# The attention branch's projection from fp16 parts, and another order of the steps ahead of it

## The chip, the cores and the metric

The kernel runs on one core of a Trainium2 chip. A core has a matrix engine (TensorE, "PE" in the profile), a vector engine (VectorE, "DVE"), a scalar engine (ScalarE, "ACT"), a general engine (GpSimd, "POOL") and a sync engine (SyncE, "SP") that here only issues transfers. Each works through its own queue of instructions in order, and semaphores tie the queues together. Operands lie in an on-chip memory of 128 partitions (SBUF); TensorE writes its sums to a second one (PSUM), from which DVE or ACT fetch them. The metric is the device time of one execution in microseconds; lower is better.

## The reference

One layer of an encoder on 1024 tokens of width 1024, all in float32. Cut to what matters:

```python
h = rmsnorm(x, norm_gain)
q, k, v, gate_a, u_in, v_in, gate_b, g_merge = split(h @ w_in)
attn = block_attention(rope(rmsnorm(q)), rope(rmsnorm(k)), v) * silu(gate_a)
y_a = attn @ w_proj_attn                                   # 512 -> 1024
vv = layernorm(gelu(v_in), ln_v_gain, ln_v_bias)
gm = gelu(u_in) * (w_spatial . vv + b_spatial) * silu(gate_b)
y_b = gm @ w_proj_gmlp                                     # 512 -> 1024
g = sigmoid(g_merge + b_merge)                             # two gates of 1024
y = g[0] * y_a + g[1] * y_b
out = rmsnorm(x + y @ w_out, final_gain)
```

There are 8 query heads and 2 key/value heads of width 64, and the attention looks at all 1024 tokens. The change concerns `y_a = attn @ w_proj_attn`, and the order of everything up to there.

## The kernel before

**Parts.** Every product is made from two parts of each operand: a hi part, the value rounded to a narrower type, and a lo part, the rest. `mm3` (lines 183 to 186) issues three matmuls for each pair: hi by hi, hi by lo, lo by hi. In most of the kernel the parts are fp16. As fp16 has a small range, an operand is scaled first: its squares are summed on ACT (`activation(..., Square, accum_out=...)`), a small matmul sums them over the partitions, and POOL takes them to the power of -1/2 (`unit_scale`, line 276; `scales`, line 325). `split16` (line 288) then makes hi on ACT with that scale and lo on DVE with one instruction. The factor is taken out again where the product is used. In two places, the projections of the branches, the parts are fp32r, four bytes wide, and need no scale: `split` (line 127) rounds on ACT and subtracts on DVE.

**Stages.** (1) x is loaded and split, k and v are projected, then the input of the spatial mixer (`v_group`). (2) The weights of q are scaled and split (`prep_q`), x is normalised (`norm_part`) and split again (`norm_split`), q is projected (`q_group`), normalised and turned (`q_norm`), and transposed (`q_split`). (3) 64 steps of attention: `scores` makes the softmax of 128 queries of one head and sends its parts through a transposing DMA, `mix2` multiplies them with v. Between them stand 24 `run_fill`, the products for the gated paths u, a and b, each from weights that `prep_next` has loaded and split. Path a ends in `gat`, the gated attention, four tiles of two halves. (4) `proj_b`, 8 times: the other branch's projection, from a stream of weights, with its loads in the tiles `wraw`. (5) Eight gates (`gate`, line 984), and among them four times `proj_a` (line 988), the attention branch's projection, two blocks of 128 output rows at a time. (6) The output product with the residual and the last norm.

**The projection.** `proj_a` calls `proj_pair`, and that calls `seven`: a product of 2 by 2 blocks in seven products instead of eight, from sums and differences of the blocks. `make_forms` makes the seven forms of `gat`; `sums` those of the weights; the function `weights` inside `proj_pair` splits each form of 256 columns just before its product. Each product has two parts of the inner dimension, and so six matmuls of 128x512. When a projection and a gate for the same rows are there, `merge` (line 888) joins them with the branch b in `ys`. The squares of the result (line 997) go into the scale of the output product.

**Order.** The order of the calls from line 1001 on is written out by hand. The framework's planner takes it as a priority and puts each engine's instructions in order by its own estimate of when operands are ready; a tile with several buffers waits until one is free. The loads are issued on SP's queue in that order, those of the early scales on ACT's. The tiles `X`, `T16`, `rB` and `vS` hold the forms of `gat`; `wraw` has four buffers, which the loads of `scales`, `proj_b`, `proj_pair` and `square_out` share.

Of the kernel before, what the change touches and what calls it, by code (L numbers as in the profile page):

```python
# [30 lines left out]
def hybrid_block_kernel(  # L31
# [681 lines left out]

    def make_forms(q, n, alloc, B, e_sub, e_hi, e_lo):
# [59 lines left out]
    GAT = ("X", "X", "T16 T16", "T16 T16", "X", "X", "rB vS")  # L774
# [14 lines left out]

    def g_tile(key, i):  # L790
        if GAT[i] == "X":
            t = tX(f"gf{key}").rearrange("p k (j t) -> p k j t", j=2)
            return t[:, 0], t[:, 1]
        return [t4(GAT[i].split()[p], f"gf{key}{p}", F32R).rearrange("p (j t) -> p j t", j=2) for p in range(2)]

# [51 lines left out]
    def proj_pair(i, b, G, dst):  # L847
# [5 lines left out]
        def weights(key, raw):  # L853
            t = sb.tile([P, 2, 256], F32R, tag="wh", bufs=WHB, name=f"wp{b}{i}{key}")
            split(t[:, 0], t[:, 1], raw, act, WPL[count[0] % len(WPL)])
            count[0] += 1
            return t[:, 0], t[:, 1]
# [131 lines left out]
    def proj_a(i):  # L989
# [12 lines left out]
    qT = [qT2[j // 2][:, j % 2] for j in range(4)]  # L1002
    load_pair(1)
# [31 lines left out]
    early = scales(["q"] + order[:4], ["xa"] * 8)  # L1035
# [5 lines left out]
    for h in range(2):  # L1041
        dve.tensor_copy(rB[:, H(h)], rp[h])
    with tc.high_priority():
# [4 lines left out]
    load_wsp(0)  # L1048
    v_group(0)
    v_group(1)  # L1050
    load_pair(0)
    load_pair(3)
    prep_q(0)
    vss = const([P, 4], "vss")
    for h in range(2):
        act.activation(t2(f"vsq{h}"), vn[:, H(h)], AF.Square, accum_out=vss[:, h:h + 1])
    load_wsp(1)
    load_pair(2)
    scale_wsp()
    norm_part(5)  # L1060
    v_post(0)
    v_post(1)
    prep_q(1)
    ktmp = t4("vS", "ktmp")
    head_norm(kn, ktmp, 0, 8, "kf")
    norm_part(0)
    bias_term(0)
    v_group(2)
    prep_q(2)
    prep_q(3)  # L1070
    prep_q(4)
    norm_part(3)
    norm_part(2)
    v_group(3)
    rope(kn, ktmp, Ak, Bk, 8, 2)
# [9 lines left out]
    prep_q(5)  # L1085
# [4 lines left out]
    split(khl[0], khl[1], kn, act)  # L1090
    prep_q(6)
    v4 = vn.rearrange("p (t h d) -> p t h d", h=2, d=64)
    v_post(2)
    v_post(7)
    norm_part(7)
    norm_split(5)
    vS = sb.tile([P, 8, 2, 128], F16, tag="vS", bufs=1, name="vS")
    act.activation(vS[:, :, :, 0:64], v4, AF.Copy, scale=vss[:, 3:4])
    dve.scalar_tensor_tensor(out=vS[:, :, :, 64:128], in0=v4, scalar=vss[:, 3:4], in1=vS[:, :, :, 0:64],
                             op0=ALU.mult, op1=ALU.subtract)  # L1100
    v_post(3)
    norm_part(6)
    norm_split(2)
    k_transposes(1)
    norm_part(4)
    norm_split(6)
    v_post(4)
    norm_split(4)
    norm_part(1)
    spatial(0)  # L1110
    norm_split(7)
    k_transposes(2)
    norm_split(1)
    bias_term(1)
    prep_q(7)
    k_transposes(3)
    norm_split(0)
    norm_split(3)
    scales(order[4:6])
    q_group(0)  # L1120
    k_transposes(0)
    v_post(6)
    q_norm(0)
    v_post(5)
    spatial(1)
    q_split(1)
    q_split(0)
    q_group(3)
    spatial(3)
    q_group(1)  # L1130
    prep_next()
    spatial(2)
    prep_next()
    q_group(2)
    q_norm(1)
    scales(order[6:8])
    q_split(2)
    q_norm(2)
# [5 lines left out]
    q_split(3)  # L1144
    scores(*hs[3])
    prep_next()
    v_affine(1)
    q_norm(3)
    scores(*hs[4])
    v_affine(2)  # L1150
    run_fill(*halves[0])
    scores(*hs[5])
    scores(*hs[6])
    scores(*hs[7])
    q_split(4)
    q_split(5)
    prep_next()
    scores(*hs[8])
    scores(*hs[9])
    scales(order[8:10])  # L1160
    scores(*hs[10])
    scales(order[10:12])
    scores(*hs[11])
    q_split(7)
    q_split(6)
    mix2(*hs[0][:2])
    scores(*hs[12])
    mix2(*hs[4][:2])
    scores(*hs[13])
    prep_next()  # L1170
    run_fill(*halves[1])
    scores(*hs[14])
    scores(*hs[15])
    scores(*hs[16])
    run_fill(*halves[2])
    mix2(*hs[8][:2])
    scores(*hs[17])
    scores(*hs[18])
    mix2(*hs[12][:2])
    scores(*hs[19])  # L1180
    scores(*hs[20])
    scores(*hs[21])
    run_fill(*halves[3])
    scores(*hs[22])
    v_affine(0)
    scores(*hs[23])
    scores(*hs[24])
    scores(*hs[25])
    run_fill(*halves[4])
    run_fill(*halves[5])  # L1190
    prep_next()
# [3 lines left out]
    scores(*hs[26])  # L1195
    mix2(*hs[16][:2])
    mix2(*hs[20][:2])
    scores(*hs[27])
    run_fill(*halves[8])
    scores(*hs[28])  # L1200
    run_fill(*halves[9])
    v_affine(3)
    scores(*hs[29])
    scores(*hs[30])
    run_fill(*halves[10])
    scores(*hs[31])
    run_fill(*halves[11])
    prep_next()
    mix2(*hs[24][:2])
    run_fill(*halves[12])  # L1210
    mix2(*hs[28][:2])
    scores(*hs[32])
# [3 lines left out]
    scores(*hs[36])  # L1216
    scores(*hs[37])
    run_fill(*halves[13])
    run_fill(*halves[14])
    scores(*hs[38])  # L1220
    mix2(*hs[32][:2])
    scores(*hs[39])
    scores(*hs[40])
    prep_next()
    scores(*hs[41])
    prep_next()
    scores(*hs[42])
    scores(*hs[43])
    scores(*hs[44])
    scores(*hs[45])  # L1230
    scores(*hs[46])
    run_fill(*halves[15])
    scores(*hs[47])
    scores(*hs[48])
    mix2(*hs[36][:2])
    mix2(*hs[40][:2])
# [199 lines left out]
```

## Time and profile before

| | |
|---|---|
| runs | 709.68, 710.73, 712.04 us; median 710.73 |
| the profiled execution's own time | 715.41 us |
| its span, first to last instruction | 713.6 us |
| mean granted clock of TensorE | 0.986 |
| busy: PE, DVE, ACT, POOL | 686.7, 569.5, 480.1, 98.3 us |

The profile is of one execution. A line of it names engine, source line and operation, then the tiles that are written and read. A number pair behind a bar is the busy time of the group in us and the mean of one instruction in ns. "[2.59 <-DMA wraw]" is idle time of the engine before an instruction, with what ended it. Matmuls overlap, so a single one's duration is longer than the time from one to the next. In windows the granted clock is a share of full speed.

### The profile page before, as it was taken

What the parts mean: (1) busy time and instruction counts of PE and PEld (TensorE: products, weight loads), DVE (VectorE), ACT (ScalarE), POOL (GpSimd) and SP (SyncE); (2) the same over time, 40 slices, a digit from 0 to 9 for tenths busy, and PEclk for the clock granted to TensorE, in tenths of its full rate; (3) what the DMA queues carried; (4) which work ended last, traced back from release to release, by engine and by line L of the source; (5) the groups of instructions that cost most, each with busy time, mean ns of one, the idle gap of its engine ahead of it and who ended that gap; (6) DMA issues with size and microseconds to landing.
All of it is one profiled execution on the core that took longest, in us unless ns stands there. A gap on an engine that the chain in (4) does not pass through costs nothing.

```text
span 713.6 us, 12246 instructions
## 1 busy us (share of the span) xinstructions
PE 686.7 (96%) x4752; PEld 403.0 (56%) x4752; DVE 569.5 (80%) x820; ACT 480.1 (67%) x896; POOL 98.3 (14%) x118
## 2 busy tenths in 40 slices
PE   9899999989998999989999999999899999999996
PEld 8788745434555545545556885644545564444443
DVE  6469997799898997899788999888688897972233
ACT  6696788667897987788678597694674648831011
POOL 0014241353011111001101001011011102000000
PEclk9999999989999999999999999999999999999999
DMA  8993255334889998899997630520520043511202
GB/s 301 407 406 122 86 188 169 117 59 90 134 187 168 199 172 143 158 221 177 167 186 166 218 104 1 176 90 30 184 75 37 1 158 124 190 42 48 118 31 88
DMA packets 159818, 102.40 MB, mean 143 GB/s; under 512 B 136208, under 2 KB 136848, under 8 KB 159760
## 3 DMA queue, kind: packets, MB, share of 16 engines
q1 hardware_dynamic: 158320, 97.14, 53.0%
q10 hardware_dynamic: 1440, 4.47, 1.6%
q8 instruction: 37, 0.61, 0.4%
q14 instruction: 21, 0.17, 0.1%
HBM read 63.85 MB, written 4.19 MB: 95 GB/s over the span
## 4 chain that ended last, share of the span: by engine, by line
PE 55%; DVE 16%; DMA 12%; ACT 9%; issue 5%; SPq 1%; POOL 1%; POOLq 0%; ACTq 0%; DVEq 0%
DMA T<-p 6%; PE out L186 4%; PE out L185 4%; PE out L184 4%; DMA wraw<-in_wall_dram 3%; DVE p L651 3%; ACT p L650 3%; DVE nm L640 3%; PE g L184 3%; PE g L186 3%; PE g L185 3%; ACT P L644 3%; PE o L665 2%; PE yb L184 2%; PE yb L186 2%
## 5 line engine op out<-in xcount | busy, mean ns | idle before, releaser
L651 DVE SCALAR_TENSOR_TENSOR p<-P,ri,p 128x1024 f16<-128x1024 f32 x64 | 83.2, 1303 | 14.4 <-ACT p L650 13.8
L644 ACT ACTIVATE P<-s,nm 128x1024 f32<-128x1024 f32 x64 | 71.1, 1111 | 24.3 <-DVE nm L640 17.4
L640 DVE TENSOR_REDUCE nm<-s 128x1 f32<-128x1024 f32 x64 | 77.5, 1214 | 1.4 <-PE s L638 1.4
L650 ACT ACTIVATE p<-P,ri 128x1024 f16<-128x1024 f32 x64 | 72.9, 1142 | 7.8 <-DMA T<-p 5.0
L665 PEld LDWEIGHTS <-vS 128*64 128x64 f16 x1536 | 46.9, 113 | 20.3 <-issue 16.4
L665 PE MATMUL o<-T,vS 128*64 128x128 f16 x1536 | 52.5, 224 | 5.7 <-DMA T<-p 5.6
L637 PE MATMUL s<-kT,qT 128*128 128x512 f16 x128 | 49.6, 388 | 4.3 <-ACT qT L450 2.0
L638 PE MATMUL s<-kT,qT 128*128 128x512 f16 x128 | 49.5, 387 | 0.0
L185 PE MATMUL out<-wo,yhl 128*128 128x512 f16 (+2 forms) x136 | 49.5, 366 | 0.0
L186 PE MATMUL out<-wo,yhl 128*128 128x512 f16 (+2 forms) x136 | 49.3, 366 | 0.0
L184 PE MATMUL out<-wo,yhl 128*128 128x512 f16 (+2 forms) x136 | 48.8, 366 | 0.0
L956 ACT ACTIVATE sq<-xr 128x1024 f32<-128x1024 f32 x7 | 7.4, 1057 | 58.9 <-DVE xr L1365 58.5
L1365 DVE SCALAR_TENSOR_TENSOR xr<-out,osc,xr 128x1024 f32<-128x1024 f32 x7 | 9.0, 1284 | 40.8 <-PE out L186 40.8
L184 PE MATMUL g<-x,wg 128*128 128x512 f16 x96 | 36.4, 380 | 0.0
L185 PE MATMUL g<-x,wg 128*128 128x512 f16 x96 | 36.4, 379 | 0.0
L186 PE MATMUL g<-x,wg 128*128 128x512 f16 x96 | 36.3, 379 | 0.0
L282 POOL TENSOR_SCALAR scg<-scg 128x1 f32<-128x1 f32 x8 | 4.1, 513 | 194.3 <-ACT usg L281 194.3
L184 PE MATMUL yb<-gm,wh 128*128 128x512 f32 x64 | 25.4, 397 | 0.0
L184 PE MATMUL v<-nh,xhl 128*128 128x512 f32 x64 | 25.3, 395 | 0.0
L185 PE MATMUL v<-nl,xhl 128*128 128x512 f32 x64 | 25.2, 393 | 0.0
L596 POOL TENSOR_TENSOR vm<-vm,ut 128x512 f32<-128x512 f32 x8 | 14.4, 1804 | 77.3 <-DVE ut L369 42.7
L185 PE MATMUL yb<-gm,wh 128*128 128x512 f32 x64 | 24.9, 390 | 0.0
(566 smaller groups left out, 1933.5 us busy)
## 6 DMA issues: line engine op xcount, KB each, us to landing
wraw<-in_wall_dram SPq DMA_DIRECT2D x91, 256.0 KB, 3.3
graw<-in_wall_dram SPq DMA_DIRECT2D x16, 512.0 KB, 5.7
xraw<-in_xT_dram SPq DMA_DIRECT2D x13, 512.0 KB, 4.9
xn<-in_x_dram SPq DMA_DIRECT2D x8, 512.0 KB, 8.0
xp<-in_xT_dram SPq DMA_DIRECT2D x8, 512.0 KB, 7.9
wor<-in_wall_dram SPq DMA_DIRECT2D x8, 512.0 KB, 5.5
xr<-in_x_dram SPq DMA_DIRECT2D x8, 512.0 KB, 4.0
out_dram<-xr SPq DMA_DIRECT2D x7, 512.0 KB, 2.6
```

The lines of the kernel that those rows point to most:

```text
L184: pe.matmul(o, ah, bh, start=start, stop=False)
L185: pe.matmul(o, ah, bl, start=False, stop=False)
L186: pe.matmul(o, al, bh, start=False, stop=stop)
L596: pool.tensor_tensor(out=vm[:, et, H(h)], in0=vm[:, et, H(h)], in1=t, op=ALU.mult)
L637: pe.matmul(sp[:, H(hf)], qs, kT[v][:, 0, H(hf)], start=True, stop=False)
L638: pe.matmul(sp[:, H(hf)], qs, kT[v][:, 1, H(hf)], start=False, stop=True)
L640: dve.tensor_reduce(out=nm, in_=sp, axis=AX.X, op=ALU.max, negate=True)
L644: act.activation(Pt, sp, AF.Exp, bias=nm, accum_out=rsum)
L650: act.activation(hi, Pt, AF.Copy, scale=ri)
L651: dve.scalar_tensor_tensor(out=lo, in0=Pt, scalar=ri, in1=hi, op0=ALU.mult, op1=ALU.subtract)
L665: pe.matmul(ot[64 * h:64 * h + 64, C(k)], vS[:, kt, v, 64 * vl:64 * vl + 64], T[:, h, 8 * p + kt, :], start=(n == 0), stop=(n == len(parts ...
L1365: dve.scalar_tensor_tensor(out=xr[tt], in0=sps[tt], scalar=osc[:, 4:5], in1=xr[tt], op0=ALU.mult, op1=ALU.add)
```

## The change

The hi and lo parts of the attention branch's projection become fp16. For that its operands get scales: `square_proj` loads the eight weight blocks of the projection once more and sums their squares, `square_gat` sums those of the gated attention, and `scale_of` makes the scales from them. The forms of `gat` and the weights' forms are split with `split16`'s two instructions. `inva`, the product of both inverse factors, is applied in the last step of `merge` and in the squares of the result. The forms of `gat` take half the memory, and lie in other tiles. And the order of the steps ahead of the projection, and of the squares and splits among the gates, is another; no step is left out. Cut to its core:

```diff
+    def scale_of(ss, n, sc, name):
+        nscale.append(name)
+        pt = ps_oz(len(nscale), f"us{name}")
+        pe.matmul(pt[:, 0:n], mscale.broadcast_to([P, P]), ss, start=True, stop=True)
+        act.activation(pt[:, 32:32 + n], pt[:, 0:n], AF.Copy, accum_out=sc[:, 1:2])
+        pool.tensor_scalar(out=sc[:, 1:2], in0=sc[:, 1:2], scalar1=1.0, scalar2=1e-30, op0=ALU.mult, op1=ALU.add)
+        pool.tensor_tensor(out=sc[:, 0:1], in0=sc[:, 1:2], in1=mhalf[:, 0:1], op=ALU.pow)
+        pool.tensor_tensor(out=sc[:, 1:2], in0=sc[:, 1:2], in1=sc[:, 0:1], op=ALU.mult)
+    def square_proj(dt):
+        raw = load_w(W_PROJ + dt, 0)
+        act.activation(raw, raw, AF.Square, accum_out=pq[0][:, dt:dt + 1])
+    def scale_proj():
+        scale_of(pq[0][:, 0:8], 8, wps, "wp")
+    def square_gat(et):
+        for h in range(2):
+            act.activation(t2(f"aq{et}{h}"), gat[et // 2, h][:, et % 2, :], AF.Square,
+                           accum_out=gas[:, 2 * et + h:2 * et + h + 1])
+    def scale_gat():
+        scale_of(gas, 8, gasc, "gat")
+        pool.tensor_tensor(out=inva, in0=gasc[:, 1:2], in1=wps[:, 1:2], op=ALU.mult)
 ...
-            split(hi, lo, raw, e_hi[i % len(e_hi)], e_lo[i % len(e_lo)])
+            split16(hi, lo, raw, gasc[:, 0:1], "dve")
 ...
-    GAT = ("X", "X", "T16 T16", "T16 T16", "X", "X", "rB vS")
+    GAT = (("X", 0), ("X", 1), ("T16", 0), ("T16", 0), ("X", 2), ("X", 3), ("vS", 0))
 ...
-            t = sb.tile([P, 2, 256], F32R, tag="wh", bufs=WHB, name=f"wp{b}{i}{key}")
-            split(t[:, 0], t[:, 1], raw, act, WPL[count[0] % len(WPL)])
+            t = sb.tile([P, 2, 256], F16, tag="wh", bufs=WHB, name=f"wp{b}{i}{key}")
+            split16(t[:, 0], t[:, 1], raw, wps[:, 0:1], "dve")
 ...
-        dve.tensor_tensor(out=ys[dt], in0=ys[dt], in1=ga, op=ALU.add)
+        dve.scalar_tensor_tensor(out=ys[dt], in0=ga, scalar=inva, in1=ys[dt], op0=ALU.mult, op1=ALU.add)
 ...
-                act.activation(junk(f"ysq{n}"), t[:, k, H(h)], AF.Square, accum_out=ysa[:, n:n + 1])
+                act.activation(junk(f"ysq{n}"), t[:, k, H(h)], AF.Square, scale=inva, accum_out=ysa[:, n:n + 1])
```

The new order where the prediction speaks of it, first around the start of the scores, then from the last scores to the second projection ("..." where calls are left out):

```diff
+    early = scales(["q"] + order[:4], ["xa"] * 8)
+    load_wsp(0)
     load_pair(1)
 ...
     q_norm(1)
+    q_norm(2)
     scales(order[6:8])
     q_split(2)
-    q_norm(2)
+    q_split(3)
+    v_affine(2)
     scores(*hs[0])
 ...
     scores(*hs[63])
     pws[0] = pair_weights(0)
+    square_gat(0)
 ...
+    square_gat(1)
     proj_b(0)
     load_chunk(0)
-    load_chunk(1)
+    square_proj(0)
     proj_b(1)
     proj_b(2)
+    square_proj(4)
+    square_gat(2)
 ...
+    square_proj(6)
+    scale_proj()
+    scale_gat()
     proj_b(6)
     make_forms(gat, 2, g_tile, GA, ASUB, AHI, ALO)
 ...
     pws[2] = pair_weights(2)
+    square_out(3)
     pws[3] = pair_weights(3)
-    square_out(0)
     gate(2)
     proj_a(1)
-    square_out(3)
+    square_out(7)
+    square_out(0)
     gate(3)
```

More of the change, by code (lines that the diff above doesn't have):

```diff
@@ L788, in hybrid_block_kernel @@
     MORDER = "w0 g0 w1 g1 w2 A a0 g2 w3 g3 w4 a1 g4 w5 g5 w6 a2 g6 w7 a3 o g7"
+    gft = {}
     def g_tile(key, i):
[L791 to L794, printed above, removed]
+        tag, k = GAT[i]
+        if tag == "X":
+            if k // 2 not in gft:
+                gft[k // 2] = tX16(f"gf{key}")
+            t = gft[k // 2][:, k % 2]
+        else:
+            t = sb.tile([P, 2, 1024], F16, tag=tag, bufs=BUFS[tag], name=f"gf{key}")
+        return t[:, 0].rearrange("p (j t) -> p j t", j=2), t[:, 1].rearrange("p (j t) -> p j t", j=2)
     XB, xraw = {}, {}
@@ L1090, in hybrid_block_kernel @@
     split(khl[0], khl[1], kn, act)
+    v_post(1)
+    norm_part(7)
+    norm_split(5)
     prep_q(6)
-    v4 = vn.rearrange("p (t h d) -> p t h d", h=2, d=64)
     v_post(2)
     v_post(7)
[L1095 to L1100, printed above, removed]
-    v_post(3)
-    norm_part(6)
-    norm_split(2)
+    norm_part(1)
+    norm_split(2)
+    v_post(3)
+    k_transposes(3)
+    v_post(6)
+    spatial(0)
+    k_transposes(2)
+    norm_split(0)
+    norm_split(1)
+    norm_part(4)
+    v_post(4)
+    prep_q(7)
+    norm_split(4)
+    bias_term(1)
     k_transposes(1)
-    norm_part(4)
+    scales(order[4:6])
     norm_split(6)
[L1107 to L1110, printed above, removed]
+    prep_next()
+    norm_split(3)
     norm_split(7)
[L1112 to L1119, printed above, removed]
     q_group(0)
+    q_norm(0)
+    spatial(1)
     k_transposes(0)
[L1122 to L1125, printed above, removed]
     q_split(1)
     q_split(0)
+    prep_next()
     q_group(3)
@@ L1143, in hybrid_block_kernel @@
     prep_next()
-    q_split(3)
     scores(*hs[3])
     prep_next()
-    v_affine(1)
-    q_norm(3)
     scores(*hs[4])
-    v_affine(2)
-    run_fill(*halves[0])
+    prep_next()
     scores(*hs[5])
@@ L1154, in hybrid_block_kernel @@
     scores(*hs[7])
+    q_norm(3)
+    scales(order[8:10])
     q_split(4)
+    run_fill(*halves[0])
     q_split(5)
-    prep_next()
     scores(*hs[8])
+    v_affine(1)
     scores(*hs[9])
-    scales(order[8:10])
     scores(*hs[10])
     scales(order[10:12])
+    prep_next()
     scores(*hs[11])
+    q_split(6)
+    scores(*hs[12])
     q_split(7)
-    q_split(6)
     mix2(*hs[0][:2])
-    scores(*hs[12])
     mix2(*hs[4][:2])
     scores(*hs[13])
-    prep_next()
-    run_fill(*halves[1])
     scores(*hs[14])
     scores(*hs[15])
+    mix2(*hs[8][:2])
+    run_fill(*halves[1])
     scores(*hs[16])
-    run_fill(*halves[2])
-    mix2(*hs[8][:2])
     scores(*hs[17])
     scores(*hs[18])
+    v_affine(0)
     mix2(*hs[12][:2])
+    run_fill(*halves[2])
     scores(*hs[19])
     scores(*hs[20])
+    mix2(*hs[16][:2])
     scores(*hs[21])
     run_fill(*halves[3])
+    run_fill(*halves[4])
     scores(*hs[22])
-    v_affine(0)
     scores(*hs[23])
+    run_fill(*halves[5])
     scores(*hs[24])
     scores(*hs[25])
-    run_fill(*halves[4])
-    run_fill(*halves[5])
-    prep_next()
+    scores(*hs[26])
     run_fill(*halves[6])
```

135 lines of the change are left out of this document (73 added, 62 removed).

## The prediction, made before the result was known

> **What bounds the kernel now.** I read the page first, then a table of windows, then the waits, and last ACT's timeline at the one place where TensorE (PE) stands still late in the run.
>
> ```profile
> span 713.6 us, 12246 instructions
> PE 686.7 (96%) x4752; PEld 403.0 (56%) x4752; DVE 569.5 (80%) x820; ACT 480.1 (67%) x896; POOL 98.3 (14%) x118
> ```
>
> PE is busy for 686.7 of 713.6 us. Where PE never waits, a step that leaves its work alone is worth nothing. So the question is where PE waits, and what its own work there weighs. In the windows below the columns after the length are busy us of PE, weight load, DVE, ACT and POOL with their counts, then granted clock, DMA share and GB/s.
>
> ```profile
> 40.00:60.00 20.00, 20.00 (x104) 17.07 (x103) 16.65 (x30) 17.25 (x38) 3.50 (x6) 1.00 0.83 330
> 120.00:140.00 20.00, 19.25 (x145) 9.96 (x143) 13.92 (x19) 15.48 (x35) 5.63 (x5) 1.00 0.48 158
> 140.00:160.00 20.00, 16.68 (x77) 7.85 (x76) 19.54 (x31) 13.03 (x28) 9.07 (x6) 0.83 0.28 52
> 160.00:180.00 20.00, 18.27 (x177) 9.88 (x176) 19.35 (x28) 15.29 (x31) 5.57 (x6) 1.00 0.53 87
> 400.00:420.00 20.00, 20.00 (x172) 16.69 (x171) 19.08 (x30) 15.62 (x31) 0.00 (x0) 1.00 0.36 120
> 420.00:440.00 20.00, 20.00 (x92) 14.25 (x91) 19.85 (x29) 18.93 (x32) 0.00 (x0) 1.00 0.14 50
> 500.00:520.00 20.00, 17.33 (x71) 10.61 (x70) 14.00 (x23) 13.41 (x35) 0.00 (x0) 0.91 0.54 181
> 625.28:702.00 76.72, 76.72 (x357) 34.84 (x356) 28.24 (x30) 12.25 (x17) 3.27 (x6) 1.00 0.17 62
> ```
>
> Before 140 us and from 400 us to the output product at the end PE is full, but for the window at 500. At 140 to 180 us, where the scores begin, DVE is full (19.54 and 19.35 of 20) and PE is short of work: 3.32 + 1.73 us idle, and a granted clock of 0.83 in the first.
>
> The window at 500 holds the second of the four attention projections that the change rewrites. Each is 7 products of 2 parts of 3 matmuls, 42 matmuls of 128x512. These are the four in turn, then the two pieces of the second in which it stands, then 36 fp16 matmuls of a gate:
>
> ```profile
> 451.92:461.73 9.81, 9.81 (x44) 7.85 (x43) 8.85 (x16) 6.49 (x16) 0.00 (x0) 1.00 0.88 312
> 498.09:512.54 14.45, 11.78 (x44) 8.76 (x43) 9.17 (x17) 6.78 (x17) 0.00 (x0) 0.88 0.60 208
> 549.03:558.85 9.82, 9.82 (x44) 7.87 (x43) 9.27 (x17) 5.35 (x11) 0.00 (x0) 1.00 0.00 1
> 576.96:587.00 10.04, 9.99 (x44) 7.79 (x43) 9.80 (x16) 4.38 (x9) 0.00 (x0) 1.00 0.33 109
> 502.20:505.97 3.77, 1.10 (x5) 0.30 (x3) 3.48 (x6) 2.89 (x7) 0.00 (x0) 0.95 0.89 256
> 505.97:508.70 2.73, 2.73 (x7) 2.15 (x8) 1.34 (x3) 0.88 (x3) 0.00 (x0) 0.50 1.02 414
> 558.85:566.63 7.78, 7.78 (x37) 3.63 (x37) 5.86 (x8) 6.54 (x17) 0.00 (x0) 1.00 0.01 2
> ```
>
> (The counts take in one or two matmuls that lap over the edges.) The second costs 14.45 - 9.82 = 4.63 us more than its neighbours: PE first gets 1.10 us of work in 3.77, and then runs at a clock of 0.50. ACT's timeline says why:
>
> ```profile
> 500.78 0.63 ACT L910 ACTIVATE wraw<-wraw 128x512 f32<-128x512 f32 x1 [2.59 <-DMA wraw<-in_wall_dram]
> 501.31 0.19 ACT L910 ACTIVATION_READ_ACCUMULATOR wraw<-wraw 128x1 f32 x1
> 502.02 1.23 ACT L885 ACTIVATE gg<-gg,bmh,scg 128x1024 f32<-128x1024 f32 x1
> 503.15 0.56 ACT L754 COPY p1y<-y 128x512 f32<-128x512 f32 x1
> 503.62 0.40 ACT L123 CAST wp01T<-wraw 128x256 fp32r<-128x256 f32 x1
> ```
>
> A square of an output weight (L910) holds ACT for 2.59 us until its load lands. Behind it in ACT's queue stand a gate's tanh, the copy of the first product and the hi part of the next product's weights (wp01T), and PE waits for that last one.
>
> **The matmuls of the projection.** 168 matmuls go from fp32r to fp16 operands. The gate's row gives 7.78 / 36 = 0.216 us for one of fp16, so 42 take 9.07 us. Leaving the stall out (9.82 for the second), the four now take 9.81 + 9.82 + 9.82 + 10.04 = 39.49 us, against 4 x 9.07 = 36.28: at most 3.2 us are to be had. DVE may not let PE have them. It is busy for 8.85, 9.27 and 9.80 us of the three undisturbed ones, and the new split costs it more:
>
> ```profile
> L129 DVE TENSOR_TENSOR wp<-wraw,wp 128x256 fp32r<-128x256 f32 x8 | 3.2, 416 | 0.0
> L129 DVE TENSOR_TENSOR wl<-wraw,wh 128x512 fp32r<-128x512 f32 x5 | 3.4, 686 | 0.0
> L290 DVE SCALAR_TENSOR_TENSOR wg<-graw,scg,wg 128x512 f16<-128x512 f32 x2 | 1.5, 743 | 0.0
> L289 ACT ACTIVATE wg<-graw,scg 128x512 f16<-128x512 f32 x2 | 1.4, 724 | 0.0
> L123 ACT CAST wh<-wraw 128x512 fp32r<-128x512 f32 x4 | 2.5, 616 | 2.8 <-PE yb L185 2.8
> ```
>
> A lo part with a scale takes 743 against 686 ns at 512 columns; half of the 57 ns for 256 columns, seven times, is 0.2 us. Were DVE the strict bound, the four would take 9.05, 9.47, 9.47 and 10.00 = 37.99 us and the gain would be 1.5 us. But part of DVE's work there is merges, which can slide into the gates (5.86 of 7.78 us in the gate's window above). I take the middle, 2.4 us.
>
> The Trainium skill, page "TensorE: Matmul & The Clock Gate", section "Wait — 56ns, not 53.3ns?", gives a warm matmul N / 2.4 GHz + about 2.5 ns, 215.7 ns at 512 columns, and makes no exception for four-byte operands; the 0.216 us of the gate agree, the 234 ns of the projection (9.82 / 42) do not. By the page the gain of rate would be nil; that is a rival below, and these rows bear on it:
>
> ```profile
> L184 PE MATMUL yb<-gm,wh 128*128 128x512 f32 x64 | 25.4, 397 | 0.0
> L184 PE MATMUL g<-x,wg 128*128 128x512 f16 x96 | 36.4, 380 | 0.0
> ```
>
> **The stall.** Its removal is worth 4.63 us. The change takes no cause away: the loads and squares of the output weights stay. It moves them: square_out(3) now stands ahead of pair_weights(3) and of the second projection, (7) and (0) behind it. All 16 halves remain, and among the four projections one was hit. I take it as gone, with the whole 4.63 us as the other end. What would be late next is nothing: PE runs on into the gate's products, whose weights wait ready.
>
> **What is added.** Sixteen squares of 128x512 on ACT (eight of the projection's weights, eight of the gated attention), each with a read of its sum; eight loads of 256 KB on SP's queue; two scales, each a small matmul, an ACT copy and three POOL steps.
>
> ```profile
> L910 ACT ACTIVATE wraw<-wraw 128x512 f32<-128x512 f32 x16 | 9.9, 621 | 7.1 <-DMA wraw<-in_wall_dram 7.1
> L279 PE MATMUL usg<-gss,mscale x2: 169/210/252, 439.0 to 439.0; 128*128 128x4 f32 x2
> L283 POOL TENSOR_TENSOR scg<-scg,mhalf 128x1 f32<-128x1 f32 x8 | 9.8, 1226 | 0.7
> wraw<-in_wall_dram SPq DMA_DIRECT2D x91, 256.0 KB, 3.3
> 410.14 0.75 DVE L618 SCALAR_TENSOR_TENSOR gat<-ga31t,avs,og 128x512 f32<-128x512 f32 x1
> L123 ACT CAST gfT<-gat 128x1024 fp32r<-128x1024 f32 x4 | 4.1, 1049 | 2.1 <-DVE x L827 2.1
> ```
>
> On PE: two matmuls of about 0.2 us with their turn, 0.3 us in all. On ACT: 16 x 0.72 us (0.62 + 0.19 less an overlap of 0.09, as 500.78 to 501.40 would give) = 11.5 us, mostly within 390 to 440. ACT has 4.4 + 1.1 us free in 400 to 440 and more ahead of it, so the squares lie beside proj_b's matmuls, which fill PE there; I cost them at nothing. With the cover gone they are the fourth rival. On SP's queue the eight loads share wraw's four buffers with proj_b's weights and stand among the loads of x and the last transposes; DMA is at 0.36 and 0.14, and eight landings of 3.3 us, one after the other, are 26 us of 40. Nothing.
>
> The forms of the gated attention now wait for a scale. Its last input is written at 410.14 + 0.75 = 410.9 us; a square (0.8), the matmul (0.2), the copy (0.4) and the POOL steps (about 2.5, of which the power is 1.23) give 415. PE first needs them at 451.92. Seven forms at some 1.1 us on ACT and 1.3 on DVE fit in those 37 us, though two that ran earlier now come later. Nothing. The merges' factor and the scaled squares of the projection's result (0.1 us more, 16 times) stand behind the same scales and beside gates. Nothing.
>
> **The other order.** Ahead of the scores nearly every step has a new place. The eight early loads of 512 KB with their squares go ahead of the second pair of x and the tables (PE is full then, 20.00 of 20, with products that need neither); norm_part(2) and vS are earlier, one prep_next goes ahead of q_group(0), and q_norm(2), q_split(3) and v_affine(2) go ahead of the first scores, v_affine(1) and the first fill behind the eighth. Each keeps its instructions and loads. What such an order can give is read at the start of the scores:
>
> ```profile
> DVE qs L440 <- ACT qs L439: 5.7, 1, 5.7
> 126.49 0.63 ACT L341 ACTIVATE wraw<-wraw 128x512 f32<-128x512 f32 x1 [1.09 <-DMA wraw<-in_wall_dram]
> 127.63 0.63 ACT L439 CAST qs<-qst 128x512 f16<-128x512 f32 x1
> PE o L665 <- DMA T<-p: 5.6, 6, 2.4
> ```
>
> DVE stands for 5.7 us at 122 to 128 behind a cast that waits in ACT's queue behind squares and their loads; DVE is then full to 180 and PE short. The best an order can do there is to give 5.7 us back. The worst is a second stretch like 140 to 160: 3.32 us idle and 0.17 x 20 = 3.4 us of clock, 6.7 us. Moved DVE work is neither less nor more, and no row says which way it falls, so I take nothing and keep -5.7 and +6.7 for the range.
>
> **Sum.** -4.6 - 2.4 + 0.3 = -6.7 us. The profiled execution took 715.41 us, so it becomes 708.7; the runs shown have a median of 710.73, 4.7 us below it, and from that the forecast is 704.0.
>
> **The rivals.**
> - *The stall stays or comes back at another projection.* For it: the squares of wraw waited for their loads six times for 7.1 us, and nothing in the edit feeds them sooner. Against: three of four projections passed with such squares about. 710.73 - 2.4 + 0.3 = 708.6.
> - *The order gives the 5.7 us back.* For it: q_norm(2) no longer stands behind four squares. Against: q_split(2) still does. 704.0 - 5.7 = 698.3.
> - *Rate nil*, the operands' width not being the cause of the 234 ns: -4.6 + 0.3 gives 706.4. Against it: a matmul of the other projection, fp32r too, takes 397 ns and one of a gate 380, each with its fill.
> - *Slower: ACT overflows under proj_b.* Between 400 and 440 it is busy for 34.6 of 40 us. If all squares fall there (11.5), with the displaced form (1.05) and the scaled copies (7 x 0.1), 7.8 us do not fit; DVE, at 38.9 of 40, cannot make up for it, and the gates' weights come late. With the clock at half for 2.73 us after each of two gaps (2 x 1.4) that is 10.6 us: 714.6. It decides from 9 us on. Against it: the squares of the first three quarters can run before 400. By the same page of the Trainium skill, section "Part 1: The HAM clock gate", half clock needs an idle window of about 3.4 us; here gaps that leave 1.10 us of work in 3.77 were enough; by the page the 2.8 us would fall away and 711.8 be left.
>
> **How the numbers follow.** Forecast 0.40, stall stays 0.22, order gives 0.20, rate nil 0.04, ACT overflows 0.14. What this kernel's measurement can tell from no change is 0.3%, 2.1 us: faster is below 708.6, slower above 712.9. The forecast, the order and the nil rate are faster (0.64), the stall's 708.6 lies on the bound and is halved (0.11 each): faster 0.75. Of the overflow 0.02 falls short: same 0.13, slower 0.12. The range runs from the order's 698.3, less 0.8 if PE gets its whole 3.2 us and 2.8 if half of PE's waits for the transposes go too (5.6 us in the row above), 694.7, so 695, to the forecast with the bad end of the order, 704.0 + 6.7 = 710.7, so 711.
>
> **What would show it.** 42 matmuls of a projection in 9.1 to 9.5 us and none near 14 show the two gains; a row of PE waiting for wp after ACT shows the first rival. DVE's wait for the cast of qs gone, and more than 17 us of PE in 140 to 160, show the second; PE below 20 with ACT at 20 between 400 and 440 the last. The forecast is wrong if PE's busy time falls by much more or less than 3 us, or if the order moves the start of proj_b by more than 7 us.

## The result, and the profile after

The change made the kernel slower by 0.8%. Timed on the same chip, the kernel after has a median of 716.32 us (714.93 to 717.52, four runs), the kernel before 710.89 us; the ratio is 1.0081, with a 95% interval of 1.0058 to 1.0104. The prediction was 704.0 us, faster, with 711 as the upper end of its range: the sign was wrong, and the time lies above the range. The profiled execution of after took 717.52 us, its span 715.7 us.

The first lines of its page, which answer to those of before:

```profile
span 715.7 us, 12299 instructions
...
PE 684.2 (96%) x4756; PEld 384.3 (54%) x4756; DVE 572.6 (80%) x820; ACT 494.0 (69%) x932; POOL 98.5 (14%) x125
```

PE has 2.5 us less work than before and the span is 2.1 us longer, so PE stands still for longer. The next table of windows has, for after, the two windows of 20 us that the prediction spoke of, then the 36 matmuls of the first gate (`g0T`), then the four attention projections in turn. Its columns are those of the prediction's windows.

```profile
140.00:160.00 20.00, 16.68 (x77) 7.33 (x75) 18.98 (x31) 12.10 (x28) 9.76 (x6) 0.83 0.28 52
420.00:440.00 20.00, 18.44 (x86) 12.68 (x84) 16.64 (x22) 19.24 (x36) 2.28 (x7) 1.00 0.27 90
438.15:448.08 9.93, 8.12 (x36) 3.38 (x37) 9.93 (x14) 6.36 (x10) 3.18 (x4) 1.00 0.01 2
453.26:462.81 9.55, 9.32 (x44) 3.87 (x43) 9.45 (x18) 5.77 (x10) 0.00 (x0) 1.00 0.27 94
499.34:508.41 9.07, 9.07 (x44) 4.06 (x43) 8.57 (x15) 4.91 (x9) 0.00 (x0) 1.00 0.35 133
545.46:559.43 13.97, 10.17 (x43) 3.62 (x44) 12.64 (x24) 11.98 (x27) 0.00 (x0) 1.00 0.63 223
578.18:588.16 9.98, 9.46 (x43) 4.03 (x42) 9.79 (x15) 4.86 (x9) 0.00 (x0) 1.00 0.21 58
```

- The second projection, which held the stall, now takes 9.07 us, just the 42 x 0.216 us that was hoped for. But the third takes 13.97 us instead of 9.82: a stall stands there now.
- The first and the last projection gain 0.26 and 0.06 us, not 0.75: DVE is busy for 9.45 of 9.55 us and for 9.79 of 9.98.
- The first gate takes 9.93 us where 36 x 0.216 = 7.78 would do, with DVE busy for all of it.
- At 140 to 160 us PE is busy for 16.68 us with a clock of 0.83, both as before. The order gave nothing there.

What PE waited for behind the attention, in the waits of after between 400 and 600 us (total, times, longest):

```profile
PE y02T L184 <- ACT wp02T L289: 2.3, 2, 1.2
PE g0T L186 <- DVE wg0T L290: 1.8, 2, 1.3
PE y02T L184 <- DVE ya L779: 0.9, 1, 0.9
PE y L186 <- DVE wp L290: 0.5, 1, 0.5
PE y02T L186 <- DVE wp02T L290: 0.5, 1, 0.5
```

ACT's timeline of after inside the third projection shows what its weights wait behind (six lines of it). L943 is the square of an output weight, L910 before.

```profile
551.90 0.62 ACT L943 ACTIVATE wraw<-wraw 128x512 f32<-128x512 f32 x1
552.42 0.19 ACT L943 ACTIVATION_READ_ACCUMULATOR wraw<-wraw 128x1 f32 x1
552.51 0.50 ACT L289 ACTIVATE wp02T<-ps,pgs 128x256 f16<-128x256 f32 x1
552.91 0.62 ACT L943 ACTIVATE wraw<-wraw 128x512 f32<-128x512 f32 x1
553.43 0.19 ACT L943 ACTIVATION_READ_ACCUMULATOR wraw<-wraw 128x1 f32 x1
553.52 0.50 ACT L289 ACTIVATE wp<-ps,pgs 128x256 f16<-128x256 f32 x1
```

ACT hardly rests from 545 to 556 us, and a square stands just ahead of most of the hi parts of the third projection's weights. (At 556.1 it then waits 1.58 us for the load of one more output weight.) These squares are where the two kernels differ most. The groups of before and of after, with the duration and the first and last start in us, and after's first matmul that reads `ysb`:

```profile
L910 ACT ACTIVATE wraw<-wraw x16: 613/617/631, 457.4 to 520.7; 128x512 f32<-128x512 f32 x16
```

```profile
L943 ACT ACTIVATE wraw<-wraw x16: 613/624/631, 535.4 to 557.7; 128x512 f32<-128x512 f32 x16
L948 PE MATMUL usout<-ysb,mscale x2: 172/214/256, 534.6 to 534.6; 128*128 128x8 f32 x2
```

All sixteen squares, spread over 63 us before, now come in one row of 22 us, and the row starts 0.8 us after `ysb` has been read. The reason is in a line that the diff doesn't touch:

```python
def small(name, n=1):
    return sb.tile([P, n], F32, tag=f"sm{n}", bufs=8 if n == 1 else 3, name=name)
```

A tile of 16 floats has three buffers. Before, three such tiles are alive here: `ysb`, `ysa` and `osq`, the sums of the output weights' squares. The change adds `pgs` (the sums of `gat` and the scales) and `pq` (the sums of the projection's weights). `pq` is read at 421.0 us and gives its buffer back; `pgs` is kept to the end. With `ysb` and `ysa` that makes three, so `osq` must wait for a buffer, and with it the squares that write it.

### The profile page after: what moved, and what is told of

It reads as the page before. It is cut to its first block, busy times and chain, and to the rows that moved or that the text cites. A ratio compares the mean times of both kernels' runs of the same rounds, so it can differ in the third digit from the quotient of the medians.

```text
span 715.7 us, 12299 instructions
## 1 busy us (share of the span) xinstructions
PE 684.2 (96%) x4756; PEld 384.3 (54%) x4756; DVE 572.6 (80%) x820; ACT 494.0 (69%) x932; POOL 98.5 (14%) x125
## 4 chain that ended last, share of the span: by engine, by line
PE 50%; DVE 21%; DMA 13%; ACT 9%; issue 5%; POOL 1%; SPq 1%; POOLq 0%; ACTq 0%; DVEq 0%
DMA wraw<-in_wall_dram 5%; PE out L184 4%; PE out L185 4%; PE out L186 4%; PE o L665 3%; DMA T<-p 3%; DMA xraw<-in_xT_dram 3%; DVE nm L640 3%; DVE p L651 2%; PE g L186 2%; PE g L184 2%; PE g L185 2%; PE s L637 2%; PE s L638 2%; ACT p L650 1%
## 5 line engine op out<-in xcount | busy, mean ns | idle before, releaser
L644 ACT ACTIVATE P<-s,nm 128x1024 f32<-128x1024 f32 x64 | 71.1, 1111 | 24.0 <-DVE nm L640 15.9
L184 PE MATMUL out<-wo,yhl 128*128 128x512 f16 (+2 forms) x136 | 48.7, 366 | 0.0
L184 PE MATMUL g<-x,wg 128*128 128x512 f16 x96 | 36.4, 379 | 0.2 <-DVE ya L779 0.2
L184 PE MATMUL yb<-gm,wh 128*128 128x512 f32 x64 | 25.4, 397 | 0.0
L184 PE MATMUL v<-nh,xhl 128*128 128x512 f32 x64 | 25.3, 396 | 0.0
L571 PE MATMUL u<-x,wu 128*128 128x512 f16 x64 | 25.3, 395 | 0.0
```

Of the source, the lines that this page charges most:

```text
L184: pe.matmul(o, ah, bh, start=start, stop=False)
L571: pe.matmul(o, wh, x16[dt][:, 0, H(h)], start=(dt == 0), stop=False)
L644: act.activation(Pt, sp, AF.Exp, bias=nm, accum_out=rsum)
```

## The experiments

All runs are set against the kernel before on the same chip (its medians there lie between 709.94 and 710.43 us), and ratios carry 95% intervals. Because the order ahead of the scores moves the attention by a microsecond or more from one kernel to another, I read one more number from each trace: the stage from the last first-part matmul of the other projection (`yb`, L184) to the first matmul of the fourth attention projection (`y03T`, L184). For after the rows are these, so that the stage is 580.8 - 431.7 = 149.1 us:

```profile
L184 PE MATMUL yb<-gm,wh x64: 387/389/586, 376.3 to 431.7; 128*128 128x512 f32 x64
L184 PE MATMUL y03T<-gfT,wp03T x6: 377/379/379, 580.8 to 587.4; 128*128 128x512 f16 x6
```

**The kernel before, once more (before_again).** No edit.

> The kernel before, once more. Theory 1 (the 4.6 us stall in the second attention projection of the profiled execution was an accident of that one execution, whose own time of 715.4 us lay 4.7 us above the median of the timed runs): the 42 matmuls of the second projection take 9.8 us in this profile, and the profiled execution's own time is within 2 us of the median of 711. Theory 2 (the stall is in every execution, and something else sets the profiled one apart): the second projection takes about 14.4 us again.

710.93 us, ratio 1.0008 (0.9996 to 1.0019). Its second projection:

```profile
498.00:509.79 11.79, 10.36 (x45) 7.71 (x43) 9.03 (x17) 6.63 (x17) 0.00 (x0) 1.00 0.71 251
```

It loses 2.0 us (11.79 against 9.82), neither 4.63 nor nothing. But another place loses here instead. The whole first gate, 84 matmuls up to the first projection, took 18.10 us in before and takes 19.94 now:

```profile
431.92:451.86 19.94, 18.59 (x87) 8.27 (x87) 19.55 (x30) 13.00 (x20) 2.85 (x4) 1.00 0.01 1
```

So in these two places the same kernel loses 4.6 us in one execution and 3.8 in the other, and the stage is 145.9 us here and 146.7 in before, 0.8 apart. The spans are 2.7 us apart (710.9 and 713.6); 1.9 of that lies ahead of the last `yb` (431.2 and 433.1 us). So the 4.63 us of stall alone do not explain why the profiled execution lay 4.7 us above the median.

**Each half of the change alone (fp16_only, order_only).** The first has the functions of the change and its squares in the order of before; the second the new order with `split` and fp32r.

```diff
 # order_only, against after
-            split16(t[:, 0], t[:, 1], raw, wps[:, 0:1], "dve")
+            split(t[:, 0], t[:, 1], raw, act, WPL[count[0] % len(WPL)])
...
 # and without the calls of square_proj, square_gat, scale_proj and scale_gat
```

> The fp16 parts with their scales alone: the order of the kernel before, with the added squares beside the same steps of proj_b as in the changed kernel. Theory 1: the rate gives 2 to 3 us and the later forms of the gated attention cost 0 to 3 us ahead of the first gate: 708 to 712 us, and the changed kernel's loss is in the order. Rival (the squares and scales themselves cost it, by filling ACT ahead of the first gate and the wraw buffers): 714 us or more.

> The new order alone, with the projection of before (fp32r parts, no added squares, loads or scales). Theory 1 (the new order among the gates piles the squares of the output weights ahead of the third projection): about 714 us, a stall of some 5 us in the third projection and none in the second. Rival (the order is no loss, the new work is): 709 to 711 us and no stall of over 2 us in any projection.

fp16_only: 720.36 us, ratio 1.0146 (1.013 to 1.0162). order_only: 709.64 us, ratio 0.9992 (0.9975 to 1.0008). So the loss comes with the fp16 parts, as the rivals of both expectations had it, and the order is no part of it; beside them it even helps by 4 us. In fp16_only the squares of the output weights run from 536.0 to 558.3 us and the third projection takes 15.02 us.

**After without the squares of the output weights (after_noosq).** Their sums are a constant, and 16 loads and squares are left out.

```diff
+    dve.memset(osq, 0.5)
...
-    square_out(3)        # and the seven others
```

> The changed kernel without the loads and squares of the output weights (the 16 sums get a constant of about their value instead). Theory (those squares and their loads, in ACT's queue and in the four buffers of wraw, hold up the third projection): the third projection takes 9.1 to 9.6 us instead of 14.0, and the time falls by 4 to 6 us to 710 to 712. Rival (it is the added squares and the forms): 715 us or more, and the third projection still over 12 us.

711.39 us, ratio 1.0011 (0.9996 to 1.0026): 4.9 us less than after. The third projection takes 9.87 us; the first gate still 9.93.

**Before with one buffer fewer (before_hold).** No fp16, no added square; only the tiles of 16 floats get two buffers.

```diff
-        return sb.tile([P, n], F32, tag=f"sm{n}", bufs=8 if n == 1 else 3, name=name)
+        return sb.tile([P, n], F32, tag=f"sm{n}", bufs=8 if n == 1 else 2 if n == 16 else 3, name=name)
```

> The kernel before with two buffers instead of three for the tiles of 16 floats, so that osq must wait for ysb there too; nothing else. Theory: the squares of the output weights start at some 535 us, the third projection loses 4 to 6 us, and the time is 714 to 716. Rival (it takes the fp16 work to make a stall of it): 709 to 712 us.

714.56 us, ratio 1.0054 (1.003 to 1.0079). The squares and the third projection of before_hold:

```profile
L910 ACT ACTIVATE wraw<-wraw x16: 613/621/635, 533.0 to 557.3; 128x512 f32<-128x512 f32 x16
```

```profile
542.52:558.27 15.75, 11.51 (x44) 7.48 (x43) 11.96 (x23) 11.62 (x29) 0.00 (x0) 1.00 0.64 212
```

One buffer fewer puts the squares into the third projection and makes it stall by 5.9 us, in a kernel that has nothing else of the change. (By the ratio the time grows by less, 3.8 us, as the second projection, now clean at 9.79 us, gives its 2.0 back.) That settles what moved the stall.

**The small tiles packed (after_pack, fp16_pack, pack_forms_late).** `ysb` shares a tile with the scales and `pq` one with the sums of `gat`, so that `osq` has a buffer early; fp16_pack does the same in the order of before; pack_forms_late also moves `make_forms` behind the first gate.

```diff
-    gas, wps, gasc, inva = pgs[:, 0:8], pgs[:, 8:10], pgs[:, 10:12], pgs[:, 12:13]
+    pgy = small("pgy", 16)
+    gas, ysb, wps, gasc, inva = pgs[:, 0:8], pgy[:, 0:8], pgy[:, 8:10], pgy[:, 10:12], pgy[:, 12:13]
+    pq.append(pgs[:, 8:16])
...
-    ysb, ysa, osq = (small(n, 16) for n in ("ysb", "ysa", "osq"))
+    ysa, osq = (small(n, 16) for n in ("ysa", "osq"))
```

> The changed kernel with its small tiles packed: the sums of squares of the other projection's result (ysb) move into the tile of the scales, and those of the projection's weights into the tile of the gated attention's sums, so that three buffers of 16 floats hold all of them and the sums of the output weights (osq) get theirs early. Nothing is left out. Theory (the three buffers of these tiles were all taken, so that osq had to wait until ysb was read, and all 16 squares of the output weights fell on the third projection): the first square of an output weight runs before 470 us instead of at 535, the third projection takes 9.1 to 9.8 us instead of 14.0, and the time falls by 4 to 5 us to about 711.5. Rival (the squares cost their time wherever they stand): 715 us or more.

> The fp16 parts in the order of before, with the same packing of the small tiles. Theory: the time falls from 720.4 by 5 to 8 us, to 712 to 715, and the third projection takes under 10 us; what then stays above the kernel before (710.3) is lost ahead of the first gate, where the forms of the gated attention come late. Rival: over 717 us.

> The packed kernel (the changed one's order), with the forms of the gated attention ranked behind the first gate instead of ahead of it. Theory (ACT and DVE make the forms among the weights of the first gate, which waits 2.6 us): the first gate loses under 1 us, and the time is 1 to 3 us below the packed kernel's. Rival (the forms are then late for the first projection): the first projection loses as much, and the time is the packed kernel's or longer.

after_pack: 723.13 us, ratio 1.018 (1.0158 to 1.0203). fp16_pack: 722.46, 1.0167 (1.0145 to 1.019). pack_forms_late: 728.94, 1.0261 (1.024 to 1.0282). All are slower than after, and nothing in the three expectations names why: with `pq` in a tile that is free early, the planner moved the eight squares of the projection's weights from behind the attention into it. In after they run at 384.6 to 406.1 us; in after_pack here, the group first and then PE's waits between 295 and 345 us:

```profile
L727 ACT ACTIVATE wraw<-wraw x8: 617/629/630, 303.9 to 332.6; 128x512 f32<-128x512 f32 x8
```

```profile
PE o L665 <- DMA T<-p: 7.9, 4, 2.7
```

There PE waits 7.9 us for the transposes of the attention, against 2.0 in after, and ACT stands 4.3 us for the loads of these squares. Whether the loads hold up the transposes in the DMA engines, or the squares hold up ACT, which makes what is transposed, is not shown; the DMA share in that window is no higher (1.03, in after 1.07). The third projection of after_pack is mended (9.86 us), but its stage, 148.2 us, is only 0.9 shorter than that of after. In pack_forms_late the forms come too late for the first projection, which takes 16.98 us; its first gate, whose weights are ranked ahead of the forms, takes 18.28 us, against 21.06 in after_pack.

**Packed, with the projection's squares kept late (pack2, fp16_pack2).** `pq` has its own tile again; the scales lie in 20 bytes of their own.

```diff
-    gas, wps, gasc, inva = pgs[:, 0:8], pgs[:, 8:10], pgs[:, 10:12], pgs[:, 12:13]
+    pgc = const([P, 5], "pgc")
+    gas, ysb, wps, gasc, inva = pgs[:, 0:8], pgs[:, 8:16], pgc[:, 0:2], pgc[:, 2:4], pgc[:, 4:5]
...
-    ysb, ysa, osq = (small(n, 16) for n in ("ysb", "ysa", "osq"))
+    ysa, osq = (small(n, 16) for n in ("ysa", "osq"))
```

> The kernel after, with the sums of the output's branch (ysb) moved into the free half of the tile that holds the sums of gat, and the scales in 20 bytes of their own; the sums of the projection's squares (pq) keep their own 16-float tile, so that these squares stay behind the attention. Theory (buffers: the squares of the output weights are late only because the third 16-float buffer comes free when ysb has been read): the sixteen squares start near 460 instead of 535, the third projection takes 9.1 to 10 us instead of 13.97, the rest of the run is as after, first gate 9.9 us included: 711 to 713 us. Rival A (the stall is a surplus of ACT work in the stage, and moves wherever the squares go): a projection still loses 4 us, time 715 to 717. Rival B (the squares of the projection are hoisted into the attention again): 720 or more.

> fp16 parts and scales in the order of the kernel before, with the same packing. Theory (buffers): the squares of the output weights start near 460, the loss of 5.9 us in the third projection goes, 713.5 to 716 us against 720.4 unpacked. Rival (the fp16 forms cost that much in this order whatever the buffers): above 718 us.

pack2: 718.32 us, ratio 1.0113 (1.0095 to 1.0131). fp16_pack2: 720.4, 1.0144 (1.0125 to 1.0163), as its rival had it. My theory fell, in its second half. The buffers did what was said: in pack2 the squares start at 462.3 and the third projection takes 9.86 us. As `pq` still has a tile of 16 floats here, it was `pgs` that stood in the way. But the time did not come back. Rival A, that the loss follows the squares, accounts for a part: the gates ahead of the second projection take 1.9 us more than in after (38.46 against 36.53) and that projection 1.7 more (10.80 against 9.07). The larger part no side had named: 3.9 us in the first gate (24.80 against 20.92), which ends at 456.8 us, ahead of the first of these squares. These are windows of pack2: the first gate's matmuls ahead of `g0T`, 36 from the first of `g0T` on, the second and the third projection.

```profile
432.00:440.62 8.62, 6.07 (x28) 2.37 (x27) 8.62 (x10) 8.62 (x16) 0.00 (x0) 1.00 0.00 0
440.62:451.60 10.98, 9.64 (x36) 3.87 (x37) 10.98 (x15) 6.36 (x10) 3.18 (x4) 0.84 0.08 22
504.71:515.51 10.80, 9.41 (x44) 3.95 (x43) 8.61 (x15) 7.15 (x16) 0.00 (x0) 1.00 0.73 254
552.18:562.04 9.86, 9.23 (x44) 4.09 (x43) 9.50 (x17) 5.93 (x11) 0.00 (x0) 1.00 0.00 0
```

In the first window DVE and ACT are both busy for 8.62 of 8.62 us while PE has 6.07 us of work: the gate's weights come late. What the two engines make beside them is the forms of `gat`. These are the first three hi parts of the forms in after, in pack2 and in pack2_nosq (the next experiment), then the matmul of pack2_nosq's scale for `gat`:

```profile
L289 ACT ACTIVATE gf<-gat,pgs x3: 1135/1136/1144, 427.1 to 434.4; 128x1024 f16<-128x1024 f32 x3
L289 ACT ACTIVATE gf<-gat,pgc x3: 1135/1137/1137, 429.6 to 436.9; 128x1024 f16<-128x1024 f32 x3
L289 ACT ACTIVATE gf<-gat,pgc x3: 1133/1134/1135, 423.1 to 430.4; 128x1024 f16<-128x1024 f32 x3
L717 PE MATMUL usgat<-pgs,mscale x2: 256/256/256, 418.4 to 418.5; 128*128 128x8 f32 x2
```

The last `yb` of the three starts at 431.7, 431.3 and 428.9 us. So the forms start 4.6, 1.7 and 5.8 us ahead of it, and the first gate takes 20.92, 24.80 and 19.63 us: in these three, the later the forms, the longer the gate. That fits pack_forms_late, where the gate loses next to nothing, but here the rest of ACT's and DVE's work is later too, and no run separates the two. Why they are later in pack2 (its last square of `gat` starts at 416.0 us, that of after at 410.5) is open.

**Without the squares, one set after the other (pack2_nosq, bare, order_noosq).** pack2_nosq is pack2 with constants for the sums of squares of `gat` and of the projection's weights; it leaves out their 16 squares and 8 loads. The scales are still made from these sums, by the same matmuls, copies and POOL steps at the same place, so the forms wait for a scale as before (418.4 and 423.1 us above), and not for `gat` alone, as the expectation has it. bare leaves out the squares of the output weights as well. order_noosq is order_only, fp32r, without the squares of the output weights.

```diff
 # pack2_nosq against pack2; bare has the edit of after_noosq too, order_noosq that one alone
+    dve.memset(gas, 50.0)
+    pq.append(small("pq", 16))
+    dve.memset(pq[0][:, 0:8], 10.26)
...
-    square_gat(0)        # and the three others
-    square_proj(0)       # and the seven others
```

> The same packing, and the scales of gat and of the projection's weights from constants: the eight squares of gat, the eight loads and squares of the projection's weights are left out, so the forms of gat wait for gat alone. Theory (the first gate's 2.2 us loss comes from forms of gat that wait for the scale and then crowd DVE and ACT beside the first gate's weights): the 36 matmuls of the first gate take 7.8 to 8.3 us, total 2 to 2.5 us below the packed kernel, 709 to 710.5 us. Rival (the loss at the first gate is the fp16 forms' own DVE work, whenever the scale is known): first gate stays at 9.9 us and the time within 1 us of the packed kernel.

> The packed kernel without any of the three sets of squares: the scales of gat, of the projection's weights and of the output's weights come from constants, so 8 + 8 + 16 squares and 24 loads are left out. What is left of the change is the rate of the projections, the fp16 forms of gat and of the weights, and the order. Theory (surplus of ACT and DVE work: the squares of the output weights cost what they delay, 4 to 5 us wherever they stand beside the fp16 forms; the late forms cost 2 us): 707 to 709 us, the losses between 460 and 600 us at 2 us or less. Rival (the fp16 forms alone, at 478 and 494 ns against 418 and 408, starve the projections without any squares): 711 us or more.

> The fp32r projection in the new order, with the scale of the output's weights from a constant: their 16 loads and squares are left out. It prices the same squares where the projection is of fp32r. Theory (in fp32r the second projection and the second gate lose 1.4 us each to them): 706.5 to 707.5 us. Rival (those gaps are not the squares'): 709 to 710 us as with them.

pack2_nosq: 712.71 us, ratio 1.0041 (1.0026 to 1.0055), but the 36 matmuls of its first gate take 9.13 us, between what the two sides expected. order_noosq: 707.2 us, ratio 0.995 (0.9933 to 0.9968), as the theory said. bare: 719.62 us, ratio 1.0131 (1.0108 to 1.0155), within the rival's 711 or more, but not for its reason. The stage behind the attention is not to blame for that: bare leaves the attention late, its last `yb` at 440.5 us against 428.9 in pack2_nosq. With the squares gone the planner set the whole attention in another order (PE waits 4.2 us for `P L644` between 230 and 345 us, against 0.9). Why it chose so is open; I read of bare only what lies behind.

The whole first gate (84 matmuls), the stage from `yb` to `y03T` and the rest of the span, in us, from the starts in each trace:

| kernel | parts | squares: output weights | added squares | first gate | `yb` to `y03T` | `y03T` to the end |
|---|---|---|---|---|---|---|
| order_noosq | fp32r | none | none | 18.1 | 142.3 | 133.7 |
| order_only | fp32r | 455 to 515 | none | 18.1 | 145.8 | 133.7 |
| before_again | fp32r | 457 to 518 | none | 19.9 | 145.9 | 133.7 |
| before, as profiled | fp32r | 457 to 521 | none | 18.1 | 146.7 | 133.8 |
| before_hold | fp32r | 533 to 557 | none | 18.1 | 148.6 | 133.7 |
| bare | fp16 | none | none | 19.6 | 143.7 | 135.0 |
| after_noosq | fp16 | none | yes | 20.8 | 144.7 | 135.0 |
| pack2_nosq | fp16 | 455 to 513 | none | 19.6 | 146.9 | 135.0 |
| after | fp16 | 535 to 558 | yes | 20.9 | 149.1 | 135.0 |
| pack2 | fp16 | 462 to 520 | yes | 24.8 | 152.3 | 135.0 |

From it the 4.6 us between order_only and after (284.1 against 279.5 for both columns) divide in this way. The fp16 parts with no squares at all cost 1.4 us in the stage and 1.3 behind it (bare against order_noosq); of the stage, the first gate loses 1.5 and the gate ahead of the fourth projection 0.8, and the four projections give 1.0. The added squares cost 1.0 (after_noosq against bare), and the first gate alone loses 1.2. The squares of the output weights cost 4.4 late beside fp16 (after against after_noosq) and 3.5 early beside fp32r (order_only against order_noosq), so 0.9 more; early beside fp16 they cost 3.2 (pack2_nosq against bare). So the squares that came late make the stall one sees, but account for only about 1 us of the 4.6: at their old place they cost nearly as much, in smaller pieces.

The division goes by one profile each. The two profiles of the kernel before differ by 0.8 us in the stage and by 1.8 in the first gate, so a share of about 1 us is not settled; and bare is packed while after_noosq is not. Nor does the sum hold for other pairs: the same added squares cost 5.4 us in pack2 (against pack2_nosq), 5.2 of them in the first gate, where the forms start late.

The 1.3 us at the end go with the fp16 parts (fp16_only, in the order of before, has 135.0 there too) and lie in the order in which DVE takes its last steps. In the fp32r kernels the last evictions (of 384 and 128 columns) follow PE's last matmul at once. In after PE ends at 708.0, and DVE is then at another row tile's last step. First DVE's timeline of after, then that of order_only at the same place:

```profile
707.82 1.29 DVE L992 SCALAR_TENSOR_TENSOR xr<-xr,rs,fg 128x1024 f32<-128x1024 f32 x1 [0.66 <-POOL rs L991]
709.02 0.87 DVE L997 SCALAR_TENSOR_TENSOR xr<-out,osc,xr 128x384 f32<-128x384 f32 x2
```

```profile
701.73 1.28 DVE L959 SCALAR_TENSOR_TENSOR xr<-xr,rs,fg 128x1024 f32<-128x1024 f32 x1
703.78 0.88 DVE L964 SCALAR_TENSOR_TENSOR xr<-out,osc,xr 128x384 f32<-128x384 f32 x2 [0.77 <-PE out L186]
```

In after the eviction waits for DVE, in order_only DVE waits 0.77 us for PE: 1.0 us of the 1.3. No kernel that keeps the whole computation is faster than before; order_only is level with it.

## Why the prediction was wrong, step by step

**The stall, -4.63 us: the step that failed.** "I take it as gone" looked at where the calls of `square_out` stand in the listing. When the squares run is set by a buffer for `osq`, and in the changed kernel `pgs` keeps that buffer. before_hold shows that a missing buffer alone moves the squares to 533 and costs the third projection 5.9 us (15.75 against 9.82). So the stall did not go: in after these squares cost 4.4 us of the stage (against after_noosq). The size was wrong as well: the prediction saw that the profiled execution took 715.41 us and that the median lies "4.7 us below it", and it took the 4.63 us of stall from that median all the same. before_again has 2.0 us of it. What the squares cost the kernel in this order is 3.5 us of the stage, and that is won only by leaving them out (order_noosq against order_only). The first rival named what came, "comes back at another projection", with too low a time, as it too was set against the median with the other terms as gains.

**The rate, -2.4 us.** Right in its mechanism, too large in size. A projection that nothing holds takes 9.07 us of fp16. Only one in four is like that: with no disturbance (bare) they take 9.55, 9.06, 9.86 and 9.98, 38.45 us against 39.43 in order_noosq, so 1.0 us. The prediction's lower bound, DVE as the strict limit, gave 37.99 us in all; taking the middle because merges could slide into the gates gave nothing, though DVE has room there: it is busy for 31.21 and 31.02 of 36.7 us in the two long stretches of gates between the projections of bare. Why its work does not move there is not shown. Of the 1.0 us, some 0.8 is only a matter of where a projection's start is counted (last section). And the split is dearer than I had it. Of its groups between 420 and 600 us, these are the hi and lo parts of the weights in order_only, and then in after:

```profile
L123 ACT CAST wp<-wraw 128x256 fp32r<-128x256 f32 x8 | 3.3, 407 | 4.8 <-PE y L186 2.9 <-PE yb L185 0.8 <-PE y02T L186 0.5
L129 DVE TENSOR_TENSOR wp<-wraw,wp 128x256 fp32r<-128x256 f32 x8 | 3.3, 417 | 0.0
```

```profile
L289 ACT ACTIVATE wp<-wraw,pgs 128x256 f16<-128x256 f32 x8 | 3.7, 496 | 0.0
L290 DVE SCALAR_TENSOR_TENSOR wp<-wraw,pgs,wp 128x256 f16<-128x256 f32 x8 | 3.7, 479 | 2.4 <-ACT wp L289 2.4
```

A lo part costs 62 ns more, not 28 (half of 57), and a hi part, which I had not costed, 89 ns. "Rate nil" is refuted. The rule of the Trainium skill that I weighed there, page "TensorE: Matmul & The Clock Gate", section "Wait — 56ns, not 53.3ns?", gives one rate and no exception by type; the same 42 matmuls took 9.82 us in fp32r and 9.07 in fp16, and the measurement decides.

**The late forms, "Nothing".** Wrong. I had the scale at 415 us, from the last input at 410.9. In after the last square of `gat` starts at 410.5, as I had it, but the scale's matmul has its turn in PE's queue, among the products of `yb`, only at 421.1, the copy of its result has its turn on ACT at 425.2, and POOL is done at 427.2. All seven hi parts of the forms start from 427.1 us on, where in order_only four of them had started by 424.1, and each lo part takes 1.28 against 1.22 us. They fall beside the first gate's own weights, DVE is full (20.92 of 20.92 us), and the gate takes 20.92 us instead of 18.1. Not all of these 2.8 us are the scale's: with the forms 1.2 us earlier against the last `yb` (bare, pack2_nosq) 1.5 stay, and before_again, with fp32r forms, loses 1.8 in one execution. No run takes the wait for the scale away by itself, so its own price stays open. The cover that I named, up to 451.92, is not the one that counts. The forms are done at 447.4, in time for the projection at 453.26; what comes late is the gate's weights, which the same two engines make.

**The added squares, "Nothing".** In after they cost 1.0 us in the stage, in pack2 5.4, nearly all of it in the first gate. The fourth rival, ACT over its limit under proj_b, gave 714.6, near to what came, and what it described came in part: the gates' weights are late, ACT was busy for 19.24 of 20 us at 420 to 440 and PE lost 1.56 us there. But before_again, without any of the change, has ACT at 19.17 and PE at 18.65 in the same window, and the larger loss of after sat in the third projection 120 us later. The clock of 0.50 which it priced did not come back: it is 1.00 in every window of after above but that at 140.

**The order, nothing.** Right as to the time: order_only is level with before (0.9992), PE is as busy at 140 to 160 us as it was (16.68 us in after), and DVE still waits 5.1 us for the cast of qs, 5.7 before. One sign that the prediction set against itself did come, a move of proj_b's start by more than 7 us: the first `yb` starts at 376.3 instead of 386.4. But the last one starts only 1.4 us earlier, and the time did not follow.

**Two scale matmuls, +0.3.** Nothing in the runs contradicts it; beside the other terms it doesn't matter. What was left out altogether is the tail, +1.0 us.

## What to carry to other kernels

Before you cost a new tile at nothing, count what else lives under its tag: with three buffers, a fourth tile of 64 bytes moved sixteen squares by 78 us. Do not take a stall of one profile from the median: the same kernel, profiled again, had 2.0 us of the 4.63 and lost 1.8 at another place. Moving work out of a stall need not win its time back: these squares cost 4.4 us late and 3.2 to 3.5 early. Price work by taking it out (a constant in its place), and look in the trace for what still waits, as the forms did for a scale made from constants. And where PE, ACT and DVE are all near full, a faster matmul is worth what the engines that feed it let through, here 1.0 of 3.2 us.

## What was not expected of the hardware

The planner's order reacts to small edits far away: leaving out squares behind the attention (bare) made the attention itself end 11.6 us later than in pack2_nosq, and freeing one small buffer (after_pack) sent eight loads into the stretch where PE waits for transposes by DMA, 7.9 us instead of 2.0. That is the framework and not the chip, but no single instruction shows it; only the starts of a stage do. Of the chip itself: in fp32r the twelve fp16 gate matmuls ahead of each projection took 2.40 us up to its first matmul, ahead of fp16 they took 2.59. The first fp32r matmul is recorded as 0.58 us long, the others as 0.39: it is recorded as starting 0.19 us sooner, not as ending sooner. So 0.19 of the 0.75 us per projection is given back at the border. And the granted clock fell to 0.84 in pack2's first gate, behind 8.62 us in which PE had 6.07 us of work, while after's third projection, with 10.17 us of work in 13.97, kept 1.00.
